# One wide product of constants ahead of each PSUM bank of the gated-delta scan and the third mixer

## The chip, the cores and the metric

The kernel runs on one core of one Trainium2 chip. The metric is the device time in microseconds of one execution, the median of three. The engines are TensorE (PE in the profile; its weight loads are PEld), VectorE (DVE), ScalarE (ACT), GpSimd (POOL) and SyncE (SP), which issues the DMAs that load. TensorE writes its results to PSUM, in banks of 128 partitions by 512 numbers.

## The reference, cut to what matters

Two blocks of a network work on 1024 tokens and 256 context tokens of width 1024. The first block projects the input, mixes it over time in three ways side by side (a long convolution called hyena, a gated linear attention called GLA, a gated delta rule called GDN), projects the concatenation back, and ends with an MLP of width 4096. The second block has two layers of windowed attention beside another recurrence. The change touches the two recurrences of the first block, GLA and GDN, each with 4 heads, run forwards and backwards, context first:

```python
# GDN, one chunk: S is the state of a head (96 x 96)
w, u = sol[..., :dk], sol[..., dk:]
v_new = u - w @ s
attn = jnp.einsum('bhid,bhjd->bhij', qc, kc) * jnp.exp(jnp.where(incl, diff, -jnp.inf))
o = (qc * jnp.exp(gcum)[..., None]) @ s + attn @ v_new
s_new = jnp.exp(g_last)[..., None] * s + jnp.einsum(
    'bhjd,bhje->bhde', kc * jnp.exp(g_last - gcum)[..., None], v_new)
...
# GLA, one chunk: a decay per channel (48), values of 96
attn = jnp.einsum('bhid,bhjd,bhijd->bhij', qc, kc, decay)
o = jnp.einsum('bhid,bhde->bhie', qc * jnp.exp(b), s) + jnp.einsum('bhij,bhje->bhie', attn, vc)
s_new = jnp.exp(b_last[:, :, 0, :])[..., None] * s + jnp.einsum(
    'bhjd,bhje->bhde', kc * jnp.exp(b_last - b), vc)
```

## The kernel before

Tokens are cut into ten chunks of 128, two of context and eight of the sequence. `block1` builds the first block in the order: projections with GDN's preparation between them, the GDN scan, the long convolution, GLA, the output projection, the MLP. What runs when is decided by a scheduler, which takes the whole program as it was written and orders each engine's instructions by a simulated timeline of its own. So GDN's scan, the convolution and the first half of GLA overlap on every engine. Each engine runs its instructions strictly in the order that results, and waits at an instruction whose operands aren't there.

**The GDN scan** (`gdn_scan`, `gdn_lane`). Two lanes run in turns, one with heads 0 and 2, one with 1 and 3. Of each head first the rows of `k`, the decays (`gdn_decay`: one product of the identity `identR` with a mask, 128x512, one of `gm`, 128x512, and four narrow ones into the same bank) and the attention of the eight chunks are made; then come ten steps, for both directions at once. A step has up to three banks, taken by `pair()`: in the first, `G` times the state `S` (row `px<-S,G` in the trace), which VectorE adds to `W` (L1323); in the second, `kw` times the new `W` (`px<-W,kw`), from which VectorE makes the next state (L271, L1330); in the third the outputs, `qs` times `S` and `at` times `W` (`px<-S,qs`, `px<-W,at`), which ScalarE or VectorE carries to `orowsd`. The first step has no first bank, the last no second, the two context steps no third. All these products are fp32; one has two records in the trace.

**The third mixer, GLA** (`gla_mix`). Heads go in pairs, p = 0 and 1, and the sequence in halves, g = 0 and 1. `gla_states` makes the state ahead of every chunk: per direction three groups of up to four chunks, each with transposes of `kh` (tile `lk`), a copy `kr`, and a bank of sums `pu` (`px<-v,kr`). `gla_tasks` makes the attention within a chunk in eight levels: VectorE forms the differences of the running log decays (L867 to L870), ScalarE takes exponentials, GpSimd multiplies by `q` and `k`, and TensorE multiplies (`eq`, `ek`). Levels of 16 and over put small blocks into two banks `pq`; the levels 8, 4, 2, 1 and 0 take two banks `pas` each, one for each head, and VectorE copies the masked part (L901). At the end, per head, a bank `po` takes twelve products (`px<-v,at`, `px<-S,eq`, `px<-S,ek`).

Banks come from rotating pools, three in the pool `px` of the scan and three in GLA's. A bank is handed out again when its last reader has finished. The scheduler's simulated timeline sets the order on each engine; no table or due time is written by hand in this part.

Of the kernel before, what the change touches and what calls it, by code (L numbers as in the profile page):

```python
# [166 lines left out]
class Builder:  # L167
# [83 lines left out]
    def ps(self, tag="px"):  # L251
        return self.pools[tag].tile([128, 512], F32, name=self.nm(tag), tag=tag)


    def mm(self, out, a, b, start=True, stop=True):
        self.nc.tensor.matmul(out, a, b, start=start, stop=stop)  # L256

    def mm3(self, out, a, b, first, last):
        self.mm(out, a[1], b[0], first, False)
        self.mm(out, a[0], b[1], False, False)  # L260
        self.mm(out, a[0], b[0], False, last)
# [552 lines left out]
    def gla_states(self, tl, b, kT, vr, S):  # L814

        nc, V, ps = self.nc, self.nc.vector, self.ps
        for d in range(2):
            bv = b[d].rearrange("p (c t) -> p c t", t=128)
            last = bv[:, :, 127:128] if d == 0 else bv[:, :, 0:1]
            dec = tl(f"dec{d}", 1, (128, 10))  # L820
            self.act(dec, last.rearrange("p c o -> p (c o)"), AF.Exp)
            kh = tl("lk", 2, (128, 10, 128))
            V.tensor_sub(out=kh, in0=last.broadcast_to([128, 10, 128]), in1=bv)
            self.act(kh, kh, AF.Exp)
            nc.gpsimd.tensor_mul(out=kh, in0=kh, in1=kT.rearrange("p (c t) -> p c t", t=128))
            yield
            order = self.fwd_order(d)
            for g0 in range(0, 9, 4):
                cs_ = order[g0 : min(g0 + 4, 9)]
                pt = ps()  # L830
                for i, c in enumerate(cs_):
                    self.tp(pt[:, i * 128 : i * 128 + 128], kh[:, c, :])
                kr = tl("kr", 2, (128, 4, 128))
                self.act(kr[:, : len(cs_)], pt[:, : len(cs_) * 128].rearrange("p (c t) -> p c t", t=128), AF.Copy)
                pu = ps()
                for i, c in enumerate(cs_):
                    for h in range(2):
                        self.mm(pu[h * 64 : h * 64 + 64, i * 96 : i * 96 + 96], kr[:, i, h * 64 : h * 64 + 64], vr[:, c, h * 96 : h * 96 + 96])
                for i, c in enumerate(cs_):
                    nx = order[g0 + i + 1]  # L840
                    if g0 + i == 0:
                        V.tensor_copy(out=S[d][:, nx], in_=pu[:, 0:96])
                    else:
                        self.stt(S[d][:, nx], S[d][:, c], dec[:, c : c + 1], pu[:, i * 96 : i * 96 + 96], ALU.mult, ALU.add)
                yield

    def gla_tasks(self, tl, p, g, qT, kT, vr, b, S, orows):


        nc, V, ps = self.nc, self.nc.vector, self.ps  # L850
        qg = qT[:, g * 512 : g * 512 + 512]
        ck = slice(256 + g * 512, 768 + g * 512)
        kg, bf, bb = kT[:, ck], b[0][:, ck], b[1][:, ck]
        at, pq = [], []
        hs = [slice(h * 64, h * 64 + 48) for h in range(2)]
        cc = [slice(c * 128, c * 128 + 128) for c in range(4)]

        def level(lv):
            if lv:
                eq, ek = tl("eq", 3, (128, 512)), tl("ek", 3, (128, 512))  # L860
                w = lambda t: t.rearrange("p (n u s) -> p n u s", u=2, s=lv)
                lo = lambda t: w(t)[:, :, 0]
                up = lambda t: w(t)[:, :, 1]
                n = 512 // (2 * lv)
                r = lo(bf)[:, :, lv - 1 : lv].broadcast_to([128, n, lv])
                r2 = up(bb)[:, :, 0:1].broadcast_to([128, n, lv])
                V.tensor_sub(out=up(eq), in0=up(bf), in1=r)  # L867
                V.tensor_sub(out=lo(eq), in0=lo(bb), in1=r2)
                V.tensor_sub(out=lo(ek), in0=r, in1=lo(bf))
                V.tensor_sub(out=up(ek), in0=r2, in1=up(bb))  # L870
                self.act(eq, eq, AF.Exp)
                self.act(ek, ek, AF.Exp)
                nc.gpsimd.tensor_mul(out=eq, in0=eq, in1=qg)
                nc.gpsimd.tensor_mul(out=ek, in0=ek, in1=kg)
            else:
                eq, ek = tl("eq", 3, (128, 512)), kg
                self.act(eq, qg, AF.Copy, scale=2.0)

            def products():
                if lv >= 16:  # L880

                    if not pq:
                        pq.extend([ps("pq"), ps("pq")])
                    w = max(lv, 32)
                    for c in range(4):
                        for j in range(0, 128, w):
                            i = c * 128 + (j if lv < 32 else j ^ w)
                            for h in range(2):
                                self.mm(pq[h][j : j + w, i : i + w], ek[hs[h], c * 128 + j : c * 128 + j + w], eq[hs[h], i : i + w])
                    if lv == 16:  # L890
                        for h in range(2):
                            at.append(tl(f"at{h}", 2, (128, 4, 128)))
                            self.act(at[h], pq[h].rearrange("p (c t) -> p c t", t=128), AF.Copy)
                    return
                pas = [ps(), ps()]
                for c in range(4):
                    for h in range(2):
                        self.mm(pas[h][:, cc[c]], ek[hs[h], cc[c]], eq[hs[h], cc[c]])
                for h in range(2):
                    pv = pas[h].rearrange("p (c t) -> p c t", t=128)  # L900
                    V.copy_predicated(at[h], self.k[f"lm{lv}"].bitcast(U32).unsqueeze(1).broadcast_to([128, 4, 128]), pv)  # L901
            return products

        def outputs():
            qs = []
            for d in range(2):
                e = tl(("eq", "ek")[d], 3, (128, 512))
                self.act(e, b[d][:, ck], AF.Exp)
                nc.gpsimd.tensor_mul(out=e, in0=e, in1=qg)
                qs.append(e)  # L910

            def products():
                for h in range(2):
                    po = ps()
                    for c in range(4):
                        oc = po[:, c * 96 : c * 96 + 96]
                        ca = 2 + g * 4 + c
                        self.mm(oc, at[h][:, c], vr[:, ca, h * 96 : h * 96 + 96], True, False)
                        self.mm(oc, qs[0][hs[h], cc[c]], S[0][hs[h], ca], False, False)
                        self.mm(oc, qs[1][hs[h], cc[c]], S[1][hs[h], ca], False, True)  # L920
                    dst = orows[:, g * 4 : g * 4 + 4, (p * 2 + h) * 96 : (p * 2 + h) * 96 + 96]
                    self.act(dst, po[:, :384].rearrange("p (c d) -> p c d", d=96), AF.Copy)
            return products

        return [lambda lv=lv: level(lv) for lv in LEVELS] + [outputs]
# [340 lines left out]
    def gdn_lane(self, tl, dr, gt, orows, heads):  # L1266
# [1 line left out]
        nc, V = self.nc, self.nc.vector  # L1268
        C3 = lambda t: t.rearrange("p (c t) -> p c t", t=128)
        ps = self.ps  # L1270
        pair = lambda: ps()[:, :192].rearrange("p (d e) -> p d e", d=2)
        orders = [self.fwd_order(0), self.fwd_order(1)]
        for h in heads:
            kT, qT = tl("k", 1, (96, TT)), tl("st", 2, (96, T))
# [12 lines left out]
            for d in range(2):  # L1287
                a, q = tl("at", 4, (128, 8, 128)), tl("qs", 4, (96, T))
                for c0 in (0, 4):
                    p = ps()  # L1290
                    self.gdn_decay(p, gt, "rg", d, h, 2 + c0, 4, self.wmask)
                    self.act(a[:, c0 : c0 + 4], C3(p), AF.Exp)
                    p = ps()
# [7 lines left out]
            for c0 in (0, 4):  # L1301
                p = ps()
                for i in range(4):
                    c = c0 + i
# [7 lines left out]
            for step in range(10):  # L1312
# [6 lines left out]
                if S is not None:  # L1319
                    p = pair()  # L1320
# [3 lines left out]
                if step < 9:  # L1324
                    Sn = tl("S", 4, (96, 2, 96))
                    p = pair()
# [8 lines left out]
                if step >= 2:  # L1335

                    l = [c - 2 for c in cs]
                    p = pair()
# [1137 lines left out]
```

## Time and profile before

| | us |
|---|---|
| median of three runs | 3692.5 (3680.39 to 3694.14) |
| profiled execution, its own time | 3682.15 |
| its span, first to last instruction | 3680.4 |
| TensorE busy | 3336.0 (91%) |
| VectorE busy | 2266.0 (62%) |
| ScalarE busy | 1523.4 (41%) |
| GpSimd busy | 1331.9 (36%) |

The profile is of one execution. Its page gives busy times, then the span in 40 equal slices of 92 us; each digit is a busy share in tenths, and the line PEclk is the clock that TensorE was granted, in tenths of full speed (9 is 90% or more). The clock has two levels, 2.4 GHz (1.00) and 1.2 GHz (0.50), so another number is a mean over time at either. A busy TensorE is one with a product under way, also where products are narrow or follow each other slowly. Line numbers are those of the kernel before, L256 being the one line from which all products are issued and L265 that of the transposes.

### The profile page before, as it was taken

What the parts mean: (1) busy time and instruction counts of PE and PEld (TensorE: products, weight loads), DVE (VectorE), ACT (ScalarE), POOL (GpSimd) and SP (SyncE); (2) the same over time, 40 slices, a digit from 0 to 9 for tenths busy, and PEclk for the clock granted to TensorE, in tenths of its full rate; (3) what the DMA queues carried; (4) which work ended last, traced back from release to release, by engine and by line L of the source; (5) the groups of instructions that cost most, each with busy time, mean ns of one, the idle gap of its engine ahead of it and who ended that gap; (6) DMA issues with size and microseconds to landing.
All of it is one profiled execution on the core that took longest, in us unless ns stands there. A gap on an engine that the chain in (4) does not pass through costs nothing.

```text
span 3680.4 us, 53188 instructions
## 1 busy us (share of the span) xinstructions
PE 3336.0 (91%) x19802; PEld 2775.0 (75%) x19802; DVE 2266.0 (62%) x4418; ACT 1523.4 (41%) x2967; POOL 1331.9 (36%) x1162
## 2 busy tenths in 40 slices
PE   7999989768896999999999699998899999998997
PEld 5668867656775778877788588887788778876885
DVE  8783642467568365555544756665677757665776
ACT  4443345431333442222211544443565554444662
POOL 2343432564547243333412201112545501113554
PEclk9899988777655999999999899999999999998998
DMA  5433543563313352222221211112544511124444
GB/s 201 145 118 100 142 130 107 192 203 114 94 46 101 121 183 92 74 72 74 90 81 46 70 50 52 51 51 87 152 121 126 170 57 55 55 70 130 121 132 140
DMA packets 346222, 388.03 MB, mean 105 GB/s; under 512 B 58099, under 2 KB 282787, under 8 KB 345964
## 3 DMA queue, kind: packets, MB, share of 16 engines
q1 hardware_dynamic: 322380, 300.33, 27.8%
q0 software_dynamic: 23584, 84.31, 6.3%
q8 instruction: 157, 2.57, 0.3%
q14 instruction: 101, 0.83, 0.1%
HBM read 296.07 MB, written 88.49 MB: 104 GB/s over the span
## 4 chain that ended last, share of the span: by engine, by line
PE 60%; DVE 15%; issue 7%; DMA 6%; ACT 5%; POOL 4%; SPq 1%; POOLq 0%; ACTq 0%; DVEq 0%
PE pm L256 34%; PE px L256 20%; PE pa L256 2%; PE px L265 2%; PE po L256 1%; DVE ma L271 1%; PE pa L265 1%; DMA mr<-in_w_ada 1%; DMA mr<-in_w_mod 1%; DVE ac L271 1%; POOL ma L387 1%; ACT e L268 1%; ACT mr L268 1%; DVE e L287 1%; DVE x L287 1%
## 5 line engine op out<-in xcount | busy, mean ns | idle before, releaser
L256 PE MATMUL pm<-x,wh 128*128 128x512 f32 (+3 forms) x4768 | 1430.2, 381 | 1.8 <-DVE x L287 1.8
L256 PEld LDWEIGHTS pm<-x,wh 128*128 128x128 f32 (+2 forms) x4768 | 863.9, 189 | 165.1 <-issue 8.4
L256 PE MATMUL pm<-x,wl 128*128 128x512 f32 (+3 forms) x2384 | 908.5, 381 | 26.5 <-ACT u L268 19.1
L256 PEld LDWEIGHTS pm<-x,wl 128*128 128x128 f32 (+2 forms) x2384 | 450.3, 189 | 110.6 <-ACT u L268 20.3
L256 PE MATMUL pm<-wo,ch 128*128 128x512 f32 x832 | 271.0, 407 | 0.0
L287 DVE TENSOR_TENSOR wl<-wr,wh 128x1024 fp32r<-128x1024 f32 (+1 forms) x110 | 144.0, 1309 | 170.2 <-ACT wh L268 169.8
L1652 DVE TENSOR_TENSOR oa<-px,oa 128x512 f32<-128x512 f32 x240 | 162.1, 688 | 132.2 <-PE px L256 131.9
L387 POOL TENSOR_TENSOR ma<-ma,mr 128x1024 f32<-128x1024 f32 x63 | 157.3, 2497 | 171.8 <-ACT mr L268 138.0
L268 ACT ACTIVATE u<-pm 128x512 f32<-128x512 f32 (+2 forms) x204 | 108.7, 544 | 261.3 <-PE pm L256 228.1
L256 PE MATMUL px<-w2h,ml 128*128 128x512 f32 x480 | 194.8, 406 | 19.8 <-DVE ml L287 10.1
L256 PE MATMUL px<-w2h,mh 128*128 128x512 f32 x480 | 192.3, 401 | 0.0
L256 PE MATMUL px<-w2l,mh 128*128 128x512 f32 x480 | 191.9, 400 | 0.0
L256 PEld LDWEIGHTS pm<-wo,ch 128*128 128x128 f32 x832 | 161.9, 196 | 32.8
L256 PE MATMUL pm<-wo,cl 128*128 128x512 f32 x416 | 171.1, 411 | 12.8 <-POOL cl L287 9.7
L275 POOL TENSOR_SCALAR mkw<-kr,gws 128x128 f32<-128x128 f32 x144 | 77.7, 543 | 282.0 <-PE px L256 240.2
L268 ACT ACTIVATE wh<-wr 128x1024 fp32r<-128x1024 f32 (+2 forms) x138 | 143.3, 1038 | 27.2 <-PE pm L256 15.4
L2360 DVE TENSOR_REDUCE amx<-pa 128x1 f32<-128x640 f32 (+2 forms) x144 | 107.3, 745 | 73.9 <-PE pa L256 72.8
L268 ACT ACTIVATE e<-e 128x1280 f32<-128x1280 f32 (+3 forms) x126 | 134.0, 1066 | 42.2 <-DVE e L275 38.7
L268 ACT ACTIVATE P<-pa,amx 128x640 f32<-128x640 f32 (+2 forms) x144 | 105.6, 733 | 95.3 <-DVE amx L275 83.9
L268 ACT ACTIVATE w2h<-wr 128x1024 fp32r<-128x1024 f32 x32 | 33.9, 1059 | 265.3 <-PE px L256 226.2
L268 ACT ACTIVATE mr<-mr,silu_cc 128x1024 f32<-128x1024 f32 x63 | 72.3, 1149 | 141.0 <-DVE ma L271 92.0
L1550 POOL TENSOR_TENSOR xr<-or,xr 128x512 f32<-128x512 f32 x72 | 93.3, 1296 | 98.0 <-DVE or L1549 80.9
(895 smaller groups left out, 7137.6 us busy)
## 6 DMA issues: line engine op xcount, KB each, us to landing
wr<-in_w_in SPq DMA_DIRECT2D x102, 512.0 KB
wr<-in_w_mlp SPq DMA_DIRECT2D x64, 512.0 KB
mr<-in_w_ada SPq DMA_DIRECT2D x48, 512.0 KB
mr<-in_w_mod SPq DMA_DIRECT2D x32, 512.0 KB
wr<-in_w_out SPq DMA_DIRECT2D x24, 512.0 KB
TF<-in_dft SPq DMA_DIRECT2D x54, 192.0 KB
rb<-npd SPq DMA_DIRECT2D x16, 640.0 KB
wr<-qd SPq DMA_DIRECT2D x36, 256.0 KB
```

Of the source, the lines that this page charges most:

```text
L256: self.nc.tensor.matmul(out, a, b, start=start, stop=stop)
L265: self.nc.tensor.transpose(out, in_, self.ident[:p, :p])
L268: self.nc.scalar.activation(out, in_, f, **kw)
L271: self.nc.vector.scalar_tensor_tensor(out=out, in0=in0, scalar=scalar, in1=in1, op0=op0, op1=op1)
L275: (eng or self.nc.vector).tensor_scalar(out=out, in0=in0, scalar1=s1, scalar2=s2, op0=op0, **kw)
L287: (leng or self.nc.vector).tensor_sub(out=lo, in0=src, in1=hi.bitcast(F32))
L387: nc.gpsimd.tensor_add(out=acc[v], in0=acc[v], in1=raw)
L1550: nc.gpsimd.tensor_add(out=xr[:, fs], in0=r, in1=xr[:, fs])
L1652: V.tensor_add(out=oa[t][:, fs], in0=p, in1=oa[t][:, fs])
L2360: V.reduce_max(m_, s[:, w0:768], axis=AX.X)
```

## The change

Ahead of a bank's own products, one product of the 128x128 identity by the identity repeated four times is put into the whole bank. It is a single-pass product (the identity is kept in the type F32R), 128 rows by 512 columns. Nothing reads its result: the bank's first own products start new sums and overwrite it. It is added for the sums of GLA's states, the banks of the levels under 16, GLA's output banks and the three banks of a GDN step. Since five lines were added, line numbers above 257 are five higher afterwards.

```diff
+    def busy(self, p):
+
+        self.mm(p.rearrange("p (c t) -> p c t", t=128), self.identR, self.identR.unsqueeze(1).broadcast_to([128, 4, 128]))
+        return p
...
-                pu = ps()
+                pu = self.busy(ps())
...
-                pas = [ps(), ps()]
+                pas = [self.busy(ps()) for _ in range(2)]
...
-                    po = ps()
+                    po = self.busy(ps())
...
-        pair = lambda: ps()[:, :192].rearrange("p (d e) -> p d e", d=2)
+        pair = lambda: self.busy(ps())[:, :192].rearrange("p (d e) -> p d e", d=2)
```

The scheduler then orders the program anew. On TensorE, a step of the second lane's first head reads so before; `S`, `G`, `W`, `kw`, `qs` and `at` are as above, and the last two rows begin the decays of another head:

```order
L256 MATMUL px_7079<-S_7044,G_7074 128x96 x2
L256 MATMUL px_7084<-W_7073,kw_6698 96x96 x2
L256 MATMUL px_7089<-S_7044,qs_6738 128x96
L256 MATMUL px_7089<-W_7073,at_6737 128x96
L256 MATMUL px_7089<-S_7044,qs_6791 128x96
L256 MATMUL px_7089<-W_7073,at_6790 128x96
L256 MATMUL px_7097<-wmask,identR 128x512
L256 MATMUL px_7097<-gm,gnng_488_1978 128x512
```

And the same step now, on the same engine:

```order
L256 MATMUL px_7117<-identR 128x512
L256 MATMUL px_7117<-S_7080,G_7112 128x96 x2
L256 MATMUL px_7123<-identR 128x512
L256 MATMUL px_7129<-identR 128x512
L256 MATMUL px_7129<-S_7080,qs_6744 128x96
L256 MATMUL px_7123<-W_7111,kw_6701 96x96 x2
L256 MATMUL px_7129<-W_7111,at_6743 128x96
L256 MATMUL px_7129<-S_7080,qs_6800 128x96
L256 MATMUL px_7129<-W_7111,at_6799 128x96
L256 MATMUL px_7138<-wmask,identR 128x512
L256 MATMUL px_7138<-gm,gnng_488_1978 128x512
```

The three products of constants stand ahead of their banks, two of them between `S,G` and the products that need the new `W`, and the first `S,qs` has moved ahead of `W,kw`.

The second place is where GLA's first sums (`v,kr`) meet the scan's last heads on TensorE. Before, they stand between the wide products of a head's decays:

```order
L256 MATMUL px_7323<-wmask,identR 128x512
L256 MATMUL px_7323<-gm,gnng_488_1978 128x512
L256 MATMUL px_7323<-gnra_1011_6086,gm 128x128 x4
L256 MATMUL px_8792<-v_8729,kr_8790 64x96 x5
L256 MATMUL px_7331<-gnra_1011_6086,gm 96x128 x4
L256 MATMUL px_8792<-v_8729,kr_8790 64x96 x2
L256 MATMUL px_7337<-wmask,identR 128x512
```

Now these decays are over by then, and the sums stand among the steps of both lanes:

```order
L256 MATMUL px_7560<-identR 128x512
L256 MATMUL px_7560<-W_7555,kw_7337 96x96 x2
L256 MATMUL px_8896<-v_8833,kr_8894 64x96 x7
L256 MATMUL px_7571<-identR 128x512
L256 MATMUL px_7571<-S_7541,G_7566 128x96 x2
L256 MATMUL px_8896<-v_8833,kr_8894 64x96
L256 MATMUL px_8927<-identR 128x512
L256 MATMUL px_8927<-v_8833,kr_8925 64x96
```

GLA's first sums have moved behind the last wide products of the scan's decays, and constants stand between them instead.

## Rows read from the trace of the kernel before

**Rows 1.** The page: span, then part 2, TensorE's busy tenths and its granted clock.

```profile
span 3680.4 us, 53188 instructions
...
PE   7999989768896999999999699998899999998997
...
PEclk9899988777655999999999899999999999998998
```

**Rows 2.** Windows, 820 to 1230 us: stretch, busy us per engine, granted clock, DMA.

```profile
820.00:856.00 36.00, 22.86 (x91) 18.82 (x92) 29.25 (x36) 7.84 (x15) 30.64 (x12) 0.59 0.35 102
856.00:900.00 44.00, 40.92 (x241) 32.39 (x239) 36.02 (x93) 9.10 (x21) 8.90 (x5) 1.00 0.47 129
900.00:924.00 24.00, 21.24 (x100) 20.19 (x100) 12.40 (x25) 4.16 (x11) 11.93 (x6) 0.51 0.31 86
924.00:938.00 14.00, 11.71 (x99) 11.05 (x99) 4.71 (x14) 5.15 (x10) 9.17 (x9) 0.99 0.57 188
958.00:996.00 38.00, 37.36 (x320) 32.65 (x321) 13.49 (x34) 13.78 (x25) 25.31 (x18) 0.50 0.12 34
996.00:1020.00 24.00, 22.53 (x224) 19.95 (x223) 20.78 (x53) 5.64 (x12) 10.20 (x8) 1.00 0.30 82
1020.00:1044.00 24.00, 23.71 (x238) 19.96 (x237) 8.48 (x20) 5.54 (x15) 6.63 (x5) 0.50 0.09 22
1044.00:1070.00 26.00, 21.24 (x112) 19.00 (x112) 24.20 (x48) 8.44 (x16) 12.72 (x11) 0.50 0.10 27
1070.00:1102.00 32.00, 31.20 (x228) 26.03 (x228) 13.20 (x33) 11.09 (x27) 15.66 (x10) 0.50 0.20 51
1102.00:1148.00 46.00, 21.98 (x218) 17.83 (x214) 42.52 (x56) 22.48 (x74) 41.30 (x28) 0.61 0.27 82
1148.00:1162.00 14.00, 13.54 (x46) 10.97 (x47) 4.07 (x5) 1.92 (x5) 4.72 (x3) 0.50 0.44 160
1220.00:1230.00 10.00, 10.00 (x48) 8.28 (x47) 3.40 (x13) 3.58 (x17) 6.10 (x7) 1.00 0.29 106
```

**Rows 3.** The chain that ended last, 820 to 1220 us, shares by line.

```profile
by line: PE px L256 46.2%; issue 8.1%; PE pm L256 3.0%; DVE ek L870 2.8%; DVE ek L869 2.3%; PE px L265 2.3%; DVE wo L287 2.1%; DVE at L901 2.1%; PE pq L256 1.9%; DVE b L800 1.9%; DMA k<-gla_k 1.9%; DVE eq L868 1.7%; DVE S L271 1.6%; DMA q<-
```

**Rows 4.** Timeline of TensorE, scan products: start, us, what; full clock, then half.

```profile
856.30 1.89 PE L256 MATMUL px<-Y,TF 128*128 128x512 f32 x6
...
858.36 0.39 PE L256 MATMUL px<-S,qs 96*128 96x96 f32 x2
858.58 0.39 PE L256 MATMUL px<-W,at 128*128 128x96 f32 x2
...
908.32 0.64 PE L256 MATMUL px<-S,qs 96*128 96x96 f32 x2
908.75 0.63 PE L256 MATMUL px<-W,at 128*128 128x96 f32 x2
```

**Rows 5.** Timeline of TensorE, wide products and the next: full clock, then half.

```profile
863.30 0.45 PE L256 MATMUL px<-wmask,identR 128*128 128x512 f32 x1
863.59 0.38 PE L256 MATMUL px<-gm,gnng 128*128 128x512 f32 x1
...
961.81 0.77 PE L256 MATMUL px<-wmask,identR 128*128 128x512 f32 x1
962.38 0.63 PE L256 MATMUL px<-gm,gnng 128*128 128x512 f32 x1
...
980.69 0.73 PE L256 MATMUL px<-wmask,identR 128*128 128x512 f32 x1
```

**Rows 6.** Groups of TensorE, 820 to 1220 us: records, busy us, mean ns, idle before.

```profile
L256 PE MATMUL px<-S,G 96*128 96x96 f32 x144 | 32.8, 367 | 8.2 <-issue 3.6 <-ACT dec L268 2.0 <-DVE S L271 1.3
L256 PE MATMUL px<-eq,ek 48*128 48x128 f32 x256 | 32.7, 380 | 4.0 <-DVE hng L271 2.1 <-DVE S L271 1.5 <-DVE at L901 0.4
L256 PE MATMUL px<-W,kw 128*96 128x96 f32 x144 | 26.8, 326 | 18.5 <-DVE W L1323 17.0 <-ACT qs L268 1.0 <-issue 0.5
L256 PE MATMUL px<-S,eq 48*128 48x96 f32 x64 | 21.4, 431 | 0.0
```

## The prediction

> **What bounds the kernel now.** I read the page first for where TensorE runs slowly: it is busy in nearly every slice, and the clock line shows a dip, 7 6 5 5 5, in slices 9 to 13, which is where the gated-delta scan and the third mixer run [rows 1]. Everywhere else the line reads 8 to 9, so a change of these two parts can only be worth something there. Second, the windows, which split 820 to 1230 us where the granted clock changes [rows 2]. The reader is to see three kinds of stretch. In 958-996, 1020-1044, 1070-1102 and 1148-1162 TensorE is busy almost throughout (37.36 of 38, 23.71 of 24, 31.20 of 32, 13.54 of 14) at a granted clock of 0.50, which is the lower of its two levels, 1.2 GHz; there TensorE at half clock is the bound. In 856-900, 924-938 and 996-1020 the clock is 0.99 to 1.00. In 820-856, 1044-1070 and 1102-1148 VectorE or GpSimd is nearly full (29.25 and 30.64 of 36; 24.20 of 26; 42.52 and 41.30 of 46) and TensorE is not. Third, the chain that ended last: of 820 to 1220 us, TensorE holds 46.2 + 3.0 + 2.3 + 1.9 = 53.4% [rows 3]. So something put in TensorE's queue at an arbitrary place there lengthens the chain with a chance of about one half. Fourth, the timeline, for what a product costs at each level: the scan's narrow products follow each other every 858.58 - 858.36 = 0.22 us at full clock and every 908.75 - 908.32 = 0.43 us at half [rows 4]. Full clock takes 0.52 of the time of half clock.
>
> **The change, part by part.** It removes nothing. It adds one product of identity by a repeated identity, 128x512, per bank: in the scan 4 heads x (9 + 9 + 8) = 104, which agrees with 144 / 4 = 36 products S,G and 36 W,kw in records of four [rows 6]; in the mixer's states 2 pairs x 2 directions x 3 = 12; in its levels below 16, 5 levels x 2 groups x 2 pairs x 2 heads = 40 (the 256 records of eq,ek over 16 a level are 16 of these 20 levels, the others take k itself); in its outputs 8, as the 64 records of S,eq over 8 say. Together 164.
>
> *What one costs.* The kernel already has the same shape, the product of the mask: the next product follows after 863.59 - 863.30 = 0.29 us at full clock and after 962.38 - 961.81 = 0.57 us at half [rows 5]. The bounds are nothing, where TensorE waits anyway, and 0.57. I take 53% of 164, 87 products, on the path: 87 x 0.29 = 25 us if all run at full clock, 87 x 0.57 = 50 us if all run at half. The other 77 are covered by waits like that for W, 17.0 us before W,kw [rows 6]: the new order puts the constants and S,qs into that wait. If the cover went, they would cost 22 us more at full clock.
>
> *What the order does.* Constants stand ahead of their bank's products, S,qs moves ahead of W,kw, and the mixer's first sums move behind the scan's last wide products. The DMAs and the other queues get the same instructions in a slightly different order up to the MLP; I price that at nothing, between -8 and +8 us (about the 10.4 us by which the runs of this kernel differ from its profiled execution), since TensorE is full there.
>
> *A wait that is added.* A constant product asks for its bank as soon as it reaches the head of the queue, before its bank's own data are there. Banks rotate in threes, so it waits for the eviction of the bank three back, and everything behind it on TensorE waits too, the other lane's products first. No row shows that wait. It lies between nothing, the eviction being a step old by then, and 17.0 us, as much as the scan waits for W now [rows 6]. I take nothing, the nearest row for an eviction that is late being of another product; it stays in the upper end of the range.
>
> *What the clock gives back.* At full clock 1020-1044 would save 0.48 x 23.71 = 11.4 us, 1070-1102 0.48 x 31.20 = 15.0, 1148-1162 6.5. In 958-996 the same would be 17.9, but GpSimd is busy 25.31 us of the 38 [rows 2], so at most 38 - 25.31 = 12.7 is to be had. All four: 45.6 us; the first three without the outputs of 1148-1162: 39.1.
>
> *Is the clock raised?* For it: in 856-900 the same scan steps run between 128x512 products of the long convolution and the clock stays at 1.00 for the whole stretch [rows 2, 4]; and right behind, in 1220-1230, wide products of weights are at 1.00. In 996-1020, once up, the clock stayed up for 24 us on narrow products alone, so it has to be lifted only at times. Against it: between 961.81 and 980.69 the kernel already has four such mask products, the first and the last shown, and the level stays 0.50 to 996 [rows 2, 5]. The scan step now gets three at a time, where those came four in 19 us. I take the clock as raised in 958-996, 1020-1044 and 1070-1102, and not in 1148-1162, where the mixer's outputs get one constant to twelve narrow products.
>
> The Trainium skill ("TensorE: Matmul & The Clock Gate", Part 1, The HAM clock gate) says that the engine is throttled by default and that a busy engine gets its full clock. Here the trace does not agree: 23.71 us busy of 24 went at 0.50 [rows 2]. Taken at its word, the rule would leave constants no way to raise the clock where the engine is already full; the sum would then be that of the first rival below.
>
> *The sum.* Constants: three quarters of the 87 at full clock, the rest at half, 65 x 0.29 + 22 x 0.57 = 31 us. Given back: 39.1. Net -8 us on the profiled execution, whose own time is 3682.15 us (span 3680.4 and 1.75 around it). The median of the runs shown is 3692.5, 10.4 us above it, so the forecast on that scale is 3692.5 - 8 = 3684 us.
>
> **The rivals.**
> First, the clock isn't raised, and the products only stand in the way. The place is the half-clock stretches of the scan; the price is 87 x 0.57 = 50 us, all added: 3742 us. For it speaks 958-996, where wide products of the same shape changed nothing; against it 856-900. It decides from the point at which less than about half of the 39.1 us comes back: 50 - 31 = 19 us dearer constants meet that loss. This is the slower side.
>
> Second, the clock is up throughout. Then all four stretches give 45.6 us, 900-924 (21.24 busy at 0.51) another 0.48 x 21.24 = 10.2, and the constants cost 25: -31 us, 3662 us. With no constant on the path it would be -56 us, 3637. For it speaks that 996-1020 holds its level unaided; against it that in 1044-1070 VectorE is full, TensorE must wait there, and the clock fell to 0.61 and 0.50 in such stretches [rows 2].
>
> Third, the clock rises but VectorE and GpSimd keep the time. In 1102-1148 they are busy 42.52 and 41.30 of 46 us: if that work is what starts the second half of the mixer, the 15.0 us saved in 1070-1102 are waited away again at its end. -8 + 15 = +7 us, 3699 us. For it speaks that TensorE idles for half of 1102-1148 already; against it that VectorE has 18.8 us free in 1070-1102 and could run ahead.
>
> **How the numbers follow.** I give the forecast 0.40, the first rival 0.25, the second 0.20, the third 0.15. A half per cent, 18 us, is about what a measurement of this kernel can tell from no change: faster is below 3674, slower above 3711. Faster is most of the second rival (0.18) and four tenths of the forecast (0.16), 0.35 rounded; slower is most of the first rival (0.23) and a little of the forecast and the third, 0.27; the rest, 0.38, is no change. The forecast's own range, with the reordering and the spread of the clock over its three stretches, is 3660 to 3708. The range reaches to -52 us, the second rival with most constants covered, and to +47 us, nearly the whole of the first: 3640 to 3740.
>
> **What would show it.** In the profile after, the constants are 128x512 products from identR alone, 164 of them, and their distance to the next row tells which level they ran at. Right, if the windows that hold the scan's last two heads and the first pair of the mixer show a clock near 1.00 and the page's dip in slices 9 to 13 is filled but for one slice; the mixer's second outputs should still be at 0.50. The first rival is right if these windows stay near 0.50 and the span from the scan's first step to the first product of the output projection grows by 40 to 50 us. The third is right if the clock is up and TensorE's idle time before products that wait for VectorE grows by what the clock gave. A wait of a constant product for an eviction, in the rows of idle time, would show the wait that I took as nothing. The forecast is wrong if the rest of the kernel, before 820 us or in the MLP, changes by more than 8 us.

## The result, and the profile after

The changed kernel takes 3727.7 us in the median (four runs, 3721.2 to 3734.7) against 3686.4 of before on the same chip (four runs): ratio 1.0116 [1.0076, 1.0156], some 43 us slower. The forecast was 3684 us; the range, 3640 to 3740, holds the time, the likeliest case does not. The profiled execution took 3734.7 us of its own, its span 3731.8.

The page after (span, TensorE's busy tenths, its granted clock) answers to [rows 1]:

```profile
span 3731.8 us, 53490 instructions
...
PE   7899989668878999999999799998899999998897
...
PEclk9999989779856799999999899999999999998998
```

The dip has moved rather than gone: slices 10 and 11 read 9 and 8 where before read 7 and 6, but slices 12 to 14 read 5, 6, 7 where before read 5, 5, 9.

Next the windows of the kernel after, cut where its clock changes, which answer to [rows 2] (stretch, its length, busy us of PE, PEld, DVE, ACT and POOL, granted clock, DMA):

```profile
863.00:962.00 99.00, 90.37 (x604) 76.07 (x602) 61.91 (x145) 23.20 (x52) 39.09 (x22) 1.00 0.51 143
962.00:986.00 24.00, 13.33 (x53) 11.22 (x53) 17.59 (x46) 7.51 (x13) 9.77 (x5) 0.50 0.07 20
986.00:1030.00 44.00, 44.00 (x464) 34.94 (x463) 23.47 (x70) 10.37 (x23) 17.28 (x14) 1.00 0.27 74
1030.00:1080.00 50.00, 48.82 (x331) 39.96 (x330) 20.56 (x44) 14.40 (x44) 15.79 (x13) 0.50 0.04 13
1080.00:1136.00 56.00, 38.04 (x159) 28.77 (x160) 52.10 (x57) 21.36 (x64) 42.14 (x29) 0.50 0.26 80
1136.00:1211.00 75.00, 65.35 (x578) 49.10 (x578) 41.45 (x71) 20.80 (x57) 35.41 (x29) 0.66 0.19 65
1211.00:1249.00 38.00, 30.62 (x97) 23.20 (x98) 16.75 (x26) 8.31 (x22) 17.61 (x16) 0.51 0.21 68
```

The clock is raised in most of the scan: 0.51 in 900-924 and 0.50 in 958-996 before, now 1.00 in all of 863-962 and 986-1030. From 1030 to 1136 it is at 0.50, though the scan runs until 1074 and constants stand there too: 38 in 986-1030, 17 in 1030-1080, 11 in 1080-1136. It isn't the mixer's levels as such that end the full clock, since 214 records of their products ran in 986-1030 at 1.00; what does is not shown. The scan's last product (`px<-W,at`) ends at 1074.0, before at 1097.7: 23.7 us gained. But the mixer's first transposes start at 981.5 (958.6), and its last `px<-v,at` ends at 1260.0 (1213.0). All that follows is late by about those 47 us: the MLP's first `px<-w2h,ml` starts at 1368.0 in place of 1320.2, and from the last `px<-v,at` to the end it takes 2471.8 us for 2467.3. So the loss has arisen by the mixer's end: the mixer starts 22.9 us later and takes 24.1 us longer, 278.5 us in place of 254.4. The late start alone is no loss, as run e1 below shows: its mixer starts at 984.6 and ends at 1217.6.

Groups of TensorE after (records, busy us, mean ns, idle before and its releasers), which answer to [rows 6]:

```profile
L256 PE MATMUL px<-identR 128*128 128x512 f32 x164 | 93.0, 590 | 25.4 <-DVE at L906 14.9 <-DVE S L276 4.0 <-DVE at L1312 3.5
L256 PE MATMUL px<-eq,ek 48*128 48x128 f32 x256 | 50.2, 386 | 0.2 <-POOL ek L879 0.2
...
L256 PE MATMUL px<-W,kw 128*96 128x96 f32 x144 | 22.4, 286 | 8.7 <-DVE W L1328 8.7
...
L256 PE MATMUL px<-eq,k 48*128 48x128 f32 x64 | 16.6, 438 | 0.0
```

The 164 constants are busy 93.0 us and idle 25.4 us before them, 14.9 of it for VectorE's masked copy (L906, formerly L901). But `px<-eq,ek`, whose 256 records are the same work, has grown from 32.7 us to 50.2, and with `px<-eq,k` (12.8 before) the levels under 16 went from 45.5 to 66.8 us. The timeline shows how. One level before, at half clock (start, us, what, records; eight products for two heads are 16 records):

```profile
1047.55 2.08 PE L256 MATMUL px<-eq,ek 48*128 48x128 f32 x16
```

And in the kernel after, at the same clock:

```profile
1222.45 2.07 PE L256 MATMUL px<-eq,ek 48*128 48x128 f32 x8
1224.45 0.79 PE L256 MATMUL px<-identR 128*128 128x512 f32 x1
1225.18 2.07 PE L256 MATMUL px<-eq,ek 48*128 48x128 f32 x8
1227.18 0.79 PE L256 MATMUL px<-identR 128*128 128x512 f32 x1
```

Before, 16 records took 2.08 us; now 8 take 2.07 (one head's alone), then comes a constant, then the other 8. Head 0's products hold rows 0 to 47 of TensorE and head 1's rows 64 to 111, and before they ran side by side. The constant of head 1's bank uses all 128 rows and stands between them.

### The profile page after: what moved, and what is told of

Read it like the earlier page. It is cut to its first block, busy times and chain, and to the rows that moved or that the text cites. A ratio compares the mean times of both kernels' runs of the same rounds, so it can differ in the third digit from the quotient of the medians.

```text
span 3731.8 us, 53490 instructions
## 1 busy us (share of the span) xinstructions
PE 3391.6 (91%) x19966; PEld 2801.5 (75%) x19966; DVE 2280.3 (61%) x4418; ACT 1520.8 (41%) x2967; POOL 1327.9 (36%) x1162
## 4 chain that ended last, share of the span: by engine, by line
PE 36%; DVE 6%; issue 3%; ACT 3%; DMA 2%; POOL 1%; SPq 0%; POOLq 0%; ACTq 0%; DVEq 0%
PE pm L256 25%; PE px L256 6%; PE pa L256 2%; PE po L256 1%; PE pa L270 1%; PE px L270 1%; ACT e L273 1%; DVE e L292 1%; DVE amx L2365 0%; DMA wr<-qd 0%; DVE x L292 0%; DVE or L1554 0%; DVE ntm L309 0%; DMA u<-kd 0%; POOL wl L292 0%
## 5 line engine op out<-in xcount | busy, mean ns | idle before, releaser
L256 PE MATMUL px<-w2h,ml 128*128 128x512 f32 x480 | 195.1, 406 | 16.6 <-DVE ml L292 13.2
L273 ACT ACTIVATE w2h<-wr 128x1024 fp32r<-128x1024 f32 x32 | 33.9, 1060 | 266.4 <-PE px L256 223.2
```

The costliest lines, as they stand in the source:

```text
L273: self.nc.scalar.activation(out, in_, f, **kw)
```

## The experiments

Ratios are to the kernel before on the same chip, with 95% intervals. "Last W,at" and "last v,at" are the ends of the scan's and the mixer's last output products in the profile, `eq,ek` the busy time of the 256 records. Theory A is that the loss is the constants' own time, B that it is their early claim of a bank and the new order, C that it is the rows they hold; the others are named in the expectations.

| run | constants | median us | ratio | last W,at | last v,at | eq,ek |
|---|---|---|---|---|---|---|
| before | none | | 1 | 1097.7 | 1213.0 | 32.7 |
| after | 164 | 3727.7 | 1.0116 [1.0076, 1.0156] | 1074.0 | 1260.0 | 50.2 |
| e1 | 104, scan | 3684.3 | 1.0007 [0.9991, 1.0023] | 1057.4 | 1217.6 | 34.1 |
| e2 | 60, mixer | 3712.6 | 1.0088 [1.0064, 1.0112] | 1120.1 | 1246.5 | 51.4 |
| e3 | 164, narrow | 3728.1 | 1.0120 [1.0096, 1.0144] | 1126.5 | 1249.8 | 55.6 |
| e4 | 40, levels | 3700.5 | 1.0048 [1.0033, 1.0063] | 1108.8 | 1229.1 | 43.4 |
| e5 | 164, levels' over own rows | 3704.3 | 1.0058 [1.0037, 1.0078] | 1053.0 | 1224.6 | 42.8 |
| e6 | 40, levels, over own rows | 3677.7 | 0.9987 [0.9973, 1.0001] | 1089.2 | 1202.3 | 34.3 |
| e8 | 20 of 128x2 between heads | 3704.2 | 1.0052 [1.0036, 1.0068] | 1111.5 | 1232.2 | 56.2 |
| e9 | none, head after head | 3681.3 | 0.9996 [0.9982, 1.0009] | 1098.4 | 1203.4 | 41.2 |
| e10 | 52, second heads | 3692.3 | 1.0022 [1.0011, 1.0033] | 1087.5 | 1214.9 | 37.1 |
| e11 | e10 and e6 | 3692.7 | 1.0027 [1.0012, 1.0041] | 1091.4 | 1217.7 | 38.6 |
| e12 | 20, states and outputs | 3693.5 | 1.0030 [1.0018, 1.0043] | 1113.9 | 1225.7 | 42.3 |
| e13 | e1 and e6 | 3706.6 | 1.0070 [1.0050, 1.0089] | 1053.8 | 1221.4 | 38.2 |
| e14 | none, less VectorE work | 3667.7 | 0.9953 [0.9937, 0.9969] | 1097.4 | 1203.8 | 34.5 |
| e15 | e1 and e14 | 3684.1 | 0.9997 [0.9985, 1.0009] | 1048.5 | 1201.6 | 37.1 |
| e16 | e5, all 2 columns wide | 3699.1 | 1.0053 [1.0033, 1.0072] | 1123.9 | 1240.8 | 51.2 |
| e17 | 164 and e14 | 3709.4 | 1.0071 [1.0044, 1.0097] | 1054.5 | 1228.2 | 45.5 |
| e19 | none, VectorE relieved | 3692.3 | 1.0036 [1.0021, 1.0051] | 1092.5 | 1202.1 | 32.2 |
| e21 | e19 and e6 | 3685.2 | 1.0017 [1.0002, 1.0032] | 1101.5 | 1214.0 | 35.4 |

### The parts alone, and their own time

e1 keeps only the constants of `pair()`, e2 only those of the mixer, e4 of these only the levels' `pas`; e3 keeps all but cuts each to two columns:

```diff
-        self.mm(p.rearrange("p (c t) -> p c t", t=128), self.identR, self.identR.unsqueeze(1).broadcast_to([128, 4, 128]))
+        self.mm(p[:, 0:2], self.identR, self.identR[:, 0:2])
```

e1: 

> Constants only ahead of the scan's 104 banks, none in the third mixer. Theory A (the mixer's 60 constants are what costs: they run at 1.2 GHz in a stretch that stays there, 0.6 to 0.7 us each on the path, while the scan gains from its own): faster than before by 10 to 30 us, the scan's last W,kw about 20 us earlier than before, clock in 863-960 near 1.00. Theory B (the new order and the wait of a constant for its bank are what costs): still 20 us or more slower than before, since the scan's constants alone already move the mixer's start behind the scan's decays.

e2: 

> Constants only in the third mixer: 12 ahead of the states' sums, 40 ahead of the levels under 16, 8 ahead of the outputs. Theory A: slower than before by 30 to 50 us, nearly the whole loss, with the clock at 0.50 from the levels of the first half on. Theory B: slower by at most 20 us, since the scan's part of the order is untouched.

e3: 

> All 164 constants, but each 128x2 in place of 128x512: same banks, same waits for a bank, next to no time of its own and no activity to hold a clock. Theory A: within 15 us of before, with the scan's clock and length as before. Theory B: keeps most of the loss, 25 us or more slower than before.

e4: 

> Only the 40 constants ahead of the two banks of each level under 16. Theory A: 40 of the mixer's 60 constants, so about two thirds of what the mixer's constants cost together, 20 to 35 us slower than before. Theory B: the levels' banks are the ones waited for (VectorE's masked copy), so as much as the mixer's constants together.

The scan's constants cost nothing measurable, the mixer's 0.9%, over half of it in the levels. So neither theory held for e1: A had it 10 to 30 us faster, B 20 us or more slower. e2, by its ratio some 32 us slower, is within A's 30 to 50; e4, some 18 us, lies under both forecasts; e3 is B's. e3 loses as much as the changed kernel without the constants' columns. It loses the raised clock too, as two windows of it show (columns as above):

```profile
947.00:1008.00 61.00, 49.41 (x370) 43.66 (x371) 26.95 (x75) 19.84 (x38) 31.97 (x18) 0.50 0.24 60
1026.00:1102.00 76.00, 76.00 (x461) 67.39 (x462) 36.63 (x86) 15.84 (x35) 23.42 (x19) 0.50 0.09 23
```

In 986-1008 the changed kernel was at 1.00, e3 at 0.50; in the second window TensorE was busy 76.00 of 76 us at 0.50. So the time of the 510 further columns and what the clock gives back about cancel, and neither is the loss. It comes from something that a constant of two columns has as well: that it stands over all rows, that it claims a bank and changes the order, or a time of its own that doesn't hang on its columns (the 164 of e3 are busy 50.8 us).

### What stands between the two heads

e5 and e6 let a level's constant use only its own head's 48 rows; e8 puts a product of 128x2 over all rows between the heads of the kernel before, e9 only changes the loops in the same way:

```diff
-                pas = [self.busy(ps()) for _ in range(2)]
+                pas = [self.busy(ps(), hs[h]) for h in range(2)]  # e5; e6 with these constants alone
...
-                for c in range(4):
-                    for h in range(2):
+                for h in range(2):
+                    if h:                                                            # e8 alone
+                        self.mm(pas[h][:, 0:2], self.identR, self.identR[:, 0:2])    # e8 alone
+                    for c in range(4):
```

e5: 

> All 164 constants as in the changed kernel, but the 40 of the mixer's levels hold only the 48 rows of their own head (48x512 in place of 128x512), same place in the program. Theory C (rows): a product over all 128 rows between the two heads of a level keeps them from running side by side (8 records of px<-eq,ek in 2.07 us in place of 16); then the levels' part of the loss goes, some 16 to 25 us of the 43: 3707 us (3698 to 3716), px<-eq,ek x256 busy 33 to 42 us. Theory B (the early claim of a bank, and the order that follows from it): count, banks and waits stay, so 3728 us (3720 to 3736), busy near 50.

e6: 

> Only the 40 constants of the levels, each over its own head's 48 rows. To be held against the same 40 over all rows, which took 3700.5 us (before 3684.8) and whose mixer ended at 1229.1. Theory C (rows): 3685 us (3680 to 3692), px<-eq,ek x256 busy 33 to 38 us, the mixer's last v,at near 1213 to 1218. Theory B (bank and order): 3700 us (3695 to 3706), busy near 50, last v,at near 1229.

e8: 

> The kernel before with no 128x512 constants; in each level under 16, head 0's products stand first, then one narrow product 128x2 over all rows into head 1's bank, then head 1's products. 20 added products of 0.01 to 0.1 us each. Theory C (rows): the heads run one after the other, 2.06 us a level at half clock and 1.0 at full, 20 levels: 3706 us (3697 to 3716), px<-eq,ek x256 busy 48 to 56 us. Theory B (early claim of a bank): the bank is claimed behind head 0's products, so nothing is held up: 3685 us (3679 to 3692). Theory A (own time of the constants): 3686 us.

e9: 

> The kernel before with nothing added; in each level under 16, head 0's four products stand first, then head 1's four, with nothing between. Theory C (rows): nothing over all rows stands between them, so head 1's begin while head 0's run, as in four levels of before at 1185 us (64 records in 9.2 us at half clock): 3686 us (3680 to 3693), px<-eq,ek x256 busy 33 to 40 us. Theory C' (it takes the alternating order itself to run side by side): 3706 us (3697 to 3716), busy 48 to 56, as with the narrow product between. Theory A, B: 3685 us.

The times of all four are those of theory C. Its other forecasts missed by a little: `eq,ek` is just above its range in e5 (42.8), e8 (56.2) and e9 (41.2), and e6's mixer ended at 1202.3, some 11 us before its range, without a gain in time. One level of e6 at half clock, two constants of 48x512 and the two heads:

```profile
1115.99 0.79 PE L256 MATMUL px<-identR 48*128 48x512 f32 x2
1116.58 1.91 PE L256 MATMUL px<-eq,ek 48*128 48x128 f32 x16
```

One of e8, where the row in the middle is the 128x2 product:

```profile
1131.92 2.07 PE L256 MATMUL px<-eq,ek 48*128 48x128 f32 x8
1133.92 0.37 PE L256 MATMUL px<-identR 128*128 128x2 f32 x1
1134.22 2.07 PE L256 MATMUL px<-eq,ek 48*128 48x128 f32 x8
1136.22 1.11 PE L270 MATMUL px<-consts,lk 128*128 128x128 f32 x4
```

And one of e9:

```profile
1118.40 3.09 PE L256 MATMUL px<-eq,ek 48*128 48x128 f32 x16
```

In e6, 1.91 us for 16 records behind two constants; in e8, 2.00 + 0.30 + 2.00 = 4.30 us from the first start to the row behind (1131.92 to 1136.22), over twice as long for one product of two columns. In e9, four products of one head and then four of the other, with nothing between, still overlap in part: 3.09 us, and where several levels follow each other more, as these rows of before show, where the order is already four and four:

```profile
1185.23 6.53 PE L256 MATMUL px<-eq,ek 48*128 48x128 f32 x45 [2.10 <-DVE hng L271]
```

45 records in 6.53 us are 0.145 each, near the 0.13 of 16 in 2.08. So the alternation counts for little (e9's time is that of before), and what counts is that no product over all rows stands between: e8 differs from e9 by those 20 products alone. The same 40 constants, in the same places of the program, cost 0.48% over all rows and nothing over their own. There the own time differs too, as the two constants of a level run side by side in e6 (0.79 us for both); in e8 it can't be much, 20 x 0.30 = 6 us of the 20.6 between e8 and e9. In the full set, own rows take the ratio from 1.0116 to 1.0058, some 21 us (5 to 38 by the two intervals), and from 1.0120 to 1.0053 where constants are two columns wide (e3, e16 below), some 25 us (13 to 36). So about half of the loss goes with the rows that the levels' constants hold. That `eq,ek` with `eq,k` grew by nearly the same, 66.8 - 45.5 = 21.3 us, is in part chance: in e5 these products still take 54.0 us (42.8 and 11.2).

The Trainium skill ("TensorEngine Tiling (Array Packing)", Tiling Modes, Key Properties) says that tiles of one tiling mode work in parallel, while a change of the mode drains TensorE. The rows of e6 and e8 agree: own rows cost nothing, and one product over all rows costs a level 4.30 - 2.08 = 2.2 us at half clock against the heads in turns, 1.2 against e9. Whether TensorE drained at that product or only had to wait for its rows, no run tells apart.

### The other half

e16 is e5 with every constant two columns wide, e12 and e13 are parts, e10 and e11 put constants only into the steps of each lane's second head:

```diff
+        pair = lambda: busy(ps())[:, :192].rearrange("p (d e) -> p d e", d=2)    # e10, e11
...
+            busy = self.busy if h != heads[0] else lambda p: p    # e10, e11
```

e10: 

> Constants only in the scan steps of each lane's second head (52), none in the mixer. The scan-only run (104) ended its scan 40 us early and yet took 3684 us, with the mixer's first transposes at 984.6 in place of 958.6; the long convolution's last products beside the first heads came 11.7 us later (VectorE t<-px,f 901.5 in place of 889.8). Theory D (constants at a clock that was up already held back the convolution, and so the mixer's start): mixer starts at 956 to 963, and takes 233 us from there as in the scan-only run, last v,at near 1192 to 1200: 3665 us (3658 to 3672). Theory E (VectorE and GpSimd keep the mixer's time whenever it starts, the third rival of the prediction): last v,at near 1210 to 1217, 3681 us (3675 to 3688).

e11: 

> The 52 constants of the scan's second heads and the 40 of the levels over their own head's 48 rows; none in states and outputs. Theories C and D: as the run with the second heads alone, or up to 5 us better, since the levels' own-row constants cost nothing alone (0.9987): 3662 us (3654 to 3672). Theory E: 3680 us (3673 to 3688). Theory F (many constants in one stretch cost more than the sum of their parts, as in the run with own rows, which was 21 us over before where its parts add to 11): 3690 us or more.

e12: 

> Only the 20 constants of the mixer's states (12) and outputs (8), over all rows. Mixer-only less levels-only was 3712.6 - 3700.5 = 12 us. Theory A here (their own time at half clock, 20 x 0.57): 11 us at most, 3690 us (3686 to 3694). Theory G (they cost only beside the levels' constants): 3681 us (3676 to 3685). Theory C (they stand between the heads of a level as well, since the levels' order before them has fewer alternations): 3695 us or more, px<-eq,ek x256 busy over 45 us.

e13: 

> All 104 constants of the scan and the 40 of the levels over their own head's 48 rows; none in states and outputs. Sum of the parts (scan only 1.0007, levels over own rows 0.9987): 3679 us (3673 to 3686), mixer's last v,at near 1215. Theory F (more than the sum, since constants of the scan then stand between a level's two heads and over all rows): 3692 us (3687 to 3700), px<-eq,ek x256 busy over 40 us.

e16: 

> All 164 constants, those of the levels over their head's 48 rows, but each 2 columns wide in place of 512: the bank claims and the order of the run with own rows (3704 us, 1.0058), without the constants' own time and without the clock that they raise in the scan. Theory H (the remaining 21 us are bank claims and order): 3703 us (3696 to 3711). Theory A (they are the constants' own time, less what the clock gives back): 3684 us (3678 to 3691), with the scan's last W,at back near 1098.

Theory D fell: with the convolution untouched the mixer started at 955.2 and yet ended at 1214.9. That is where E had it, but e10's time, 3692.3, is above E's range as well; e11 is where F had it (3690 or more). The parts don't add: e1 and e6 together should give 0.9994, and e13 measured 1.0070. That is even above F's range, while `eq,ek`, which F had over 40 us, is at 38.2; so F's reason isn't shown. Theory H's time held against A's: e16 is as slow as e5. Groups of e5, then of e16 (columns as above):

```profile
L256 PE MATMUL px<-identR 128*128 128x512 f32 (+1 forms) x164 | 89.5, 573 | 27.7 <-DVE at L906 18.7 <-DVE S L276 4.2 <-DVE at L1312 3.5
...
L256 PE MATMUL px<-eq,ek 48*128 48x128 f32 x256 | 42.8, 368 | 1.9 <-POOL ek L879 1.9
```

```profile
L256 PE MATMUL px<-identR 128*128 128x2 f32 (+1 forms) x164 | 52.4, 335 | 16.2 <-DVE S L276 7.7 <-DVE at L1312 2.2 <-ACT kw L273 1.9
L256 PE MATMUL px<-eq,ek 48*128 48x128 f32 x256 | 51.2, 432 | 0.0
```

So the rest goes with the presence of the constants and not with their columns. Three causes are left for it, and no run separates them.

The first is time that a constant takes whatever its width. e16's expectation set it at nothing, e8's at 0.01 to 0.1 us; but e16's constants are busy 52.4 us, and in e8 the row behind one starts 0.30 us later. This is theory A in another form, and e16 doesn't refute it. e12's 11 us, too, agree with the own time of its twenty wide constants, at 20 x 0.57.

The second is the claim of a bank. In e5, TensorE still waits 18.7 us with a constant at the head of its queue for VectorE's masked copy out of the bank's former user. In e16 that wait is 1.4 us and the loss the same, so this copy can't be all of it.

The third is the order, and with it the heads again. The 256 records of `eq,ek` are 1.9 at a time in e3 (256 x 0.402 us in 55.6), 2.2 in e16, 3.0 before: own rows bring only part of the pairs back, since other products stand between the heads in the new order. One such place in e16, where a constant of the states and `v,kr` follow one head's records:

```profile
1021.35 2.05 PE L256 MATMUL px<-eq,ek 48*128 48x128 f32 x8
1023.34 0.37 PE L256 MATMUL px<-identR 128*128 128x2 f32 x1
1023.63 0.59 PE L256 MATMUL px<-v,kr 128*64 128x96 f32 x4
1024.15 0.37 PE L256 MATMUL px<-identR 48*128 48x2 f32 x1
```

In e12, which has no constants in the levels, `eq,ek` is dearer than before too (42.3), so there the first and the third are not told apart either.

### Where the scan's early end went

e14, e15 and e17 take 13.4 us off VectorE by leaving out the low halves of `w_out`; e19 and e21 move them to GpSimd instead, and GpSimd's scaling of the heads to ScalarE:

```diff
-        self.split(raw, hi, lo, leng=leng)
+        if leng:                                                  # e14, e15, e17
+            self.split(raw, hi, lo, leng=leng)
+        else:
+            self.act(hi, raw, AF.Copy)
+            self.act(lo, hi.bitcast(F32), AF.Copy, scale=0.0)
...
-        self.split(raw, hi, lo, leng=leng)
+        self.split(raw, hi, lo, leng=self.nc.gpsimd)              # e19, e21
...
-            nc.gpsimd.tensor_mul(out=ov, in0=ov, in1=rs[:, c].unsqueeze(2).broadcast_to([128, 4, 96]))
+                self.act(ov, ov, AF.Copy, scale=rs[:, c, h : h + 1])   # e19, e21, per head
```

e14: 

> The kernel before, without constants; the low halves of the 8 tiles of w_out that VectorE subtracts while the mixer runs (wo<-wr,wo x8, 13.4 us of VectorE, 1099 to 1148) are left out: ScalarE writes zeros in their place (8 copies of about 1.05 us more there). Theory E (in 1102-1148, where VectorE is busy 42.5 of 46 us, it sets the time): last v,at about 8 to 13 us before 1213, 3672 us (3666 to 3677). Theory J (TensorE and the order of its queue set it there too): 3682 us (3677 to 3688). The reference for what scan-only gains from the same edit.

e15: 

> The scan-only kernel (104 constants, 3684 us, scan done 40 us early, then VectorE busy 40.0 of 40 us in 1060-1100 and TensorE 15.9) with the same low halves left out. Theory E: the 13.7 us come off the mixer, which takes up the early end of the scan: 3671 us (3665 to 3677), last v,at near 1204. Theory J: 3684 us (3679 to 3690). If e14 falls as much, the 40 us were not waiting for these copies alone.

e17: 

> The changed kernel, all 164 constants, with the low halves of w_out left out as above. In the changed kernel TensorE waited 14.9 us for VectorE's masked copies before constants, in 1079 to 1111, while VectorE did these subtractions and the scans of b. Theory E: 3714 us (3708 to 3721). Theory J: 3727 us (3721 to 3734).

e19: 

> A whole computation without constants that takes the same 13.4 us off VectorE: the low halves of w_out are subtracted on GpSimd (8 of about 2.5 us, twice the 1.27 us of its 128x512 subtractions), and GpSimd's scaling of the normed heads (16 of 0.95 us) goes to ScalarE (64 of about 0.27 us). Theory E with GpSimd within its means: as with the halves left out (0.9953), 3669 us (3662 to 3676). Rival: GpSimd, busy 41.3 of 46 us in 1102-1148, takes VectorE's place as the bound: 3684 us or more.

e21: 

> The same, with the 40 constants of the levels over their own head's 48 rows (alone 0.9987). If the two add: 3665 us (3657 to 3673). If the constants cost once VectorE no longer covers them (as the scan's did: 0.9997 against 0.9953 without VectorE's copies): 3680 us or more.

The window 1060-1100 of e1, then that of before:

```profile
1060.00:1100.00 40.00, 15.94 (x75) 13.58 (x73) 40.00 (x56) 22.00 (x82) 27.03 (x17) 0.50 0.27 87
```

```profile
1060.00:1100.00 40.00, 35.77 (x192) 29.72 (x200) 21.20 (x48) 11.69 (x21) 19.16 (x13) 0.50 0.18 47
```

With the scan done, VectorE was busy 40.00 of 40 us and TensorE 15.94; before, 21.20 and 35.77. So VectorE was full where the scan had been. Taking 13.4 us from VectorE gave e14 16.6 us: in the kernel before, VectorE is on the path there. For the changed kernel it isn't shown: e17 is at 1.0071 for 1.0116, but the two intervals overlap. In e14 1102-1148 shows it busy 29.30 us, 42.52 in [rows 2], and TensorE 27.19 for 21.98:

```profile
1102.00:1148.00 46.00, 27.19 (x213) 22.28 (x210) 29.30 (x57) 29.37 (x85) 35.65 (x28) 0.57 0.23 79
```

For e15 the expectation failed. Its mixer does end at 1201.6, 16 us before e1's, with VectorE no longer full:

```profile
1060.00:1100.00 40.00, 25.26 (x122) 20.97 (x122) 32.94 (x44) 25.22 (x75) 33.38 (x19) 0.50 0.27 77
```

Yet its median did not move, and by its own expectation this means that the 40 us weren't waiting for these copies alone: next to e14 its scan ended 48.9 us earlier and its mixer 2.2. In its profiled execution what follows the mixer (span less the last v,at) took 2476.7 us, in e1's 2467.6, in e14's 2462.4. Over all profiles here that remainder lies between 2462 and 2482, though no edit is near it; what moves it stays open, and with it where e15's 16 us went.

e19 fell too: its rival gives the right side of the time, though not its place. GpSimd's subtractions and ScalarE's scalings in it:

```profile
L287 POOL TENSOR_TENSOR wo<-wr,wo 128x1024 fp32r<-128x1024 f32 x8 | 18.8, 2369 | 0.2 <-ACT wo L268 0.2
```

```profile
L268 ACT ACTIVATE orowsl<-orowsl,hnr 128x96 f32<-128x96 f32 x32 | 8.7, 361 | 2.9 <-DVE hnr L307 2.9
```

They cost 2.37 us and 0.36 us each, and the profiled mixer ended at 1202.1, yet the median is 1.0036. The profile is of the fastest of its runs (3677.6, median 3692.3), so what is late in the others no profile shows. e21 was to tell whether e6's constants still cost nothing on top of e19; it is no slower than e19, but as e19 itself failed, its forecasts have lost their ground. No version that does all the work beats both kernels: e6 (0.9987) is not told from before.

## Why the prediction was wrong

**What bounds the kernel** was right for the scan (TensorE at half clock) and half right for the mixer: the windows showed VectorE at 42.52 of 46 us, I gave that to a rival with a chance of 0.15, and e14 shows that it was on the path in the kernel before. (Slices 9 to 13 of before read 7 7 6 5 5, not 7 6 5 5 5; no term rests on it.)

**What one costs**, 0.29 and 0.57: right in the scan (894.50 to 894.81 is 0.31 at full clock), low in the level shown, 0.73 at half (1224.45 to 1225.18). e3 and e16 are as slow without the columns, so these cost net nothing once the clock pays for them, near what the sum had (31 against 39.1); what a constant costs whatever its width is still open.

**What the order does** is the step that failed: "I price that at nothing, between -8 and +8 us". I asked what is moved and never what the new product stands between. The pairing was to be seen in the rows: 256 records of eq,ek with a mean of 380 ns are 97.3 us, done in 32.7 us busy, three at a time [rows 6], where those of S,G make 52.8 in 32.8. Twenty levels at 1 to 2 us were there to be priced. The rows of the levels' constants cost some 21 us of the loss (5 to 38), which no case of the prediction had.

**A wait that is added**, "I take nothing": the upper bound named was 17.0 us; measured are 25.4 us of idle time before constants, of which 14.9 for the mask copy. Before W,kw the wait fell from 18.5 to 8.7 us, so part of it only moved. With the order and the width-free time of a constant it is what is left for the second half of the loss, which by e16 is not the columns; the three are not separated, and the cause of that half stays open.

**Is the clock raised?** Right for most of the scan, with the stretches displaced: 986-1030 is at 1.00 throughout, and with two-column constants e3 is at 0.50 in 947-1008. Wrong for 1070-1102, which stayed at 0.50 with constants in it. The argument that a clock once up stays up on narrow products was read from 996-1020; [rows 2] also show it at 0.50 from 1020 on, with TensorE busy 23.71 of 24 us. That e1's scan ends 40.3 us early, close to the 39.1 reckoned, is in part luck: the 40.3 hold the constants' own time, which the 39.1 leave out, and the mixer, which starts 26.0 us later there, shares TensorE with the scan for 72.8 us in place of 139.1. In the changed kernel it is 23.7.

**The rivals.** The first gave nearly the time (3742), from a cause that isn't there: the scan's clock was raised. So it is luck that the range held the time. The third, 3699, named VectorE as the bound that takes a gain away; e1's VectorE was full, but e15 doesn't show that this alone kept the gain. No case had a place for the heads.

**The sum** fails on one point more: a gain of the scan was counted as a gain of the kernel. e1 has all of it, 40 us, and is at 1.0007.

## What to carry to other kernels

Before a product is put into a tight sequence, look at what runs beside it: if the records of two heads take no longer than those of one (16 in 2.08 us, 8 in 2.07), they run at once on different rows, and one product over all rows between them, were it two columns wide, ends that. If a filler must be there, give it the rows of the product it precedes; in the full set that saved about half of the loss. A filler of two columns isn't free either. And price a raised clock only as far as the stage's next bound: with the scan 40 us shorter VectorE was full, and the kernel no faster.

## What the runs showed of the hardware

The granted clock stood at 1.00 in 986-1030 with 38 constants of 512 columns among the scan's and the mixer's products, and at 0.50 in 947-1008 of e3, where the constants have two columns. A busy TensorE alone doesn't raise it: in 1030-1080 TensorE was busy 48.82 of 50 us with 17 wide constants, in e3 76.00 of 76 us, both at 0.50. A product of 128x2 delayed the next row by 0.30 us at half clock (e8). And two halves of the rows overlap without a strict alternation: 45 records in 6.53 us with four products of one head after four of the other, 16 in 2.08 us in turns.
